# Where stores, halo pages and weight sums stand: a one-core kernel of a hybrid decoder block

## The chip, the cores and the metric

The kernel runs on one core of a Trainium2 chip. The core has a matmul engine (TensorE, PE in the profile), a vector engine (VectorE, DVE), an engine for activation functions (ScalarE, ACT), GpSimd (POOL) and SyncE (SP), from whose queue all transfers of this kernel are issued. The metric is the device time of one launch in microseconds, the lower the better.

## The reference

One layer on a sequence of 2048 positions with 1024 channels, in float32: a mixer of 16 recurrent heads and 8 short-convolution groups, then a gated feed-forward part with a convolution over positions, each with a residual, and a last norm.

```python
def reference(x, norm1_g, w_in, ..., final_g):
    for l in range(DEPTH):
        h = rms_norm(x, norm1_g[l])
        z = jnp.einsum('bsd,de->bse', h, w_in[l])
        lru_x, lru_gate, sc_b, sc_c, sc_x = jnp.split(z, splits, axis=-1)
        lru_x = causal_dwconv(lru_x, lru_conv_w[l]) + lru_conv_b[l]
        y_lru = rg_lru(lru_x, ...) * jax.nn.gelu(lru_gate)
        y_sc = sc_b * causal_dwconv(sc_c * sc_x, sc_conv_w[l])
        y_mix = jnp.concatenate([y_lru, y_sc], axis=-1)
        x = x + jnp.einsum('bse,ed->bsd', y_mix, w_out[l])
        h = rms_norm(x, norm2_g[l])
        u = causal_dwconv(jnp.einsum('bsd,df->bsf', h, w_up[l]), ffn_conv_w[l])
        gate, up = jnp.split(u, 2, axis=-1)
        x = x + jnp.einsum('bsf,fd->bsd', jax.nn.gelu(gate) * up, w_down[l])
    return rms_norm(x, final_g)
```

## The kernel before

Channels lie on the 128 partitions, positions along the free axis. The sequence is worked in two halves of T = 1024 positions, each in two blocks of NB = 512. A float32 value is split into a high and a low part (`split`, L182: ACT rounds, DVE subtracts), and each product is three matmuls. One matmul has a 128x128 weight tile and 512 columns.

The program runs through four kinds of stages, each once for each half: the mixer's input products (`in_phase`, 12 units of the list `UNITS`), the output projection (`project`, two blocks of 12 steps), the up products of the feed-forward part (`up_phase`, 24 pairs of gate `ug` and value `un`), and the down products (`sweeps`). Mixer and projection of half 0 come first, then those of half 1, then up and down of half 0, then up and down of half 1. Up and down use a seven-product scheme for 2x2 blocks: seven sweeps of six steps, each step loading two pages, one of weights or their sums (L756) and one of data (L757), splitting both and issuing 24 matmuls. The sums S1 to S4 of down weights are made early, in `down_sums` (sa, sb, sc), one of twelve beside each unit of half 0's `in_phase`, and spilled to DRAM (`s_d`). The products of the up phase are combined in `up_rest` and spilled to `f_d` (B11 of an even unit alone; of an odd unit B21, B22 and T1 to T4).

What sets the order. TensorE and SP run in the order in which the program is written; DVE, ACT and POOL in an order that a scheduler sets, by priorities. SP's queue is worked in order: a store whose data isn't there holds the loads behind it. Stores therefore don't stand where their data is made: `defer(n, dst, src)` puts them on a list, each load of weights calls `tick`, which counts all down, and a store is issued once it is at the head of the list and its count is 0 or less. So n is the number of weight loads that go ahead of it.

```python
    def tick():
        for w in waiting:
            w[0] -= 1
        while waiting and waiting[0][0] <= 0:
            _, dst, src = waiting.pop(0)
            nc.sync.dma_start(dst, src)
```

Pages. `raw_tile` has two buffers, so a step's load waits until the step two before it is split. Pages of T + 3 columns (`big`) and of two blocks (`res_page`) share four buffers of the tag "u": lru inputs `xl`, the convolution product `pr`, the second half's x, the residuals `xr` of the projection, the h pages `ha` and `hb` of `h_prep`, `ug` and `un` with their halos, and one of the residuals `x2r` of half 0's sweeps ("21"; the others are from the tag "act" with 28 buffers). Sums, h's helpers and up results are from `tmp`, seven buffers.

The stores that matter here: `up_rest` defers its spills by 1, and by 3 for the last two units; `store_pair` defers the second residual stream (x2) and the third (x3, of `down0_done`) by 1; `finish_block` defers the output of half 1 by 1. `h_beside` prepares the h pages of half 1 beside steps 4, 12, 25 and 37 of half 0's sweeps. In half 1's sweeps `down1_beside` loads x3 of half 0 again (fx), scales and stores it, and after step 37 scales the second block of half 1 (L889).

Of the kernel before, what the change touches and what calls it, by code (L numbers as in the profile page):

```python
# [64 lines left out]
def block_kernel(  # L65
# [52 lines left out]
    def tmp(name):  # L118
        return page(name, "tmp", 7)

    def big(name):
        return ub.tile([P, T + 3], F32, name=name, tag="u", bufs=4)

    def raw_tile(name):
        return sb.tile([P, 6, NB], F32, name=name, tag="wr", bufs=2)
# [134 lines left out]
            nc.vector.scalar_tensor_tensor(acc, acc, 1.5, y, ALU.add, ALU.mult)  # L260
        return acc

    def with_halo(name, n, half, store):
        t = big(name)
        if half == 0:
            nc.gpsimd.memset(t[:, 0:n], 0.0)
        else:
            nc.gpsimd.tensor_copy(t[:, 0:n], store)
        return t
# [81 lines left out]
    def sc_first(s, half, acts, rs, ps):  # L351
        cc = flat(act(f"cc{half}_{s}"))
        evac(cc, ps, rs)
        ps = in_product(24 + s, half, acts)
        pr = with_halo(f"pr{half}_{s}", 2, half, p_halo[:, s, :])
        evac(pr[:, 2 : 2 + T], ps, rs)
        nc.vector.tensor_tensor(pr[:, 2 : 2 + T], pr[:, 2 : 2 + T], cc, ALU.mult)
        keep_halo(pr, 2, half, p_halo[:, s, :])
        return pr
# [8 lines left out]
        return cv  # L368

    def x_prep(half, k, parts=1):  # L370
        x = (flat(act(f"x{half}_{k}")) if half == 0 else big(f"x{half}_{k}"))[:, :T]
        hi = flat(act(f"xh{half}_{k}"))
        lo = flat(act(f"xl{half}_{k}"))
        g = col(O_G1 + k)
        n = T // parts
        for i in range(parts):
            ts = slice(i * n, (i + 1) * n)
            nc.sync.dma_start(x[:, ts], xT[k, :, half * T + i * n : half * T + (i + 1) * n])
            nc.scalar.activation(r32(hi[:, ts]), x[:, ts], AF.Copy, scale=g)
            nc.vector.scalar_tensor_tensor(r32(lo[:, ts]), x[:, ts], g, hi[:, ts], ALU.mult, ALU.subtract)  # L380
        return hi, lo, x
# [136 lines left out]
            nc.vector.tensor_tensor(a, a, sq[:, 0, :], ALU.add)  # L518
            nc.vector.tensor_tensor(a, a, sq[:, 1, :], ALU.add)

    def res_page(name):
        return ub.tile([P, 2, NB], F32, name=name, tag="u", bufs=4)

    def x_residual(half):
        def get(t, i):
            r = res_page(f"xr{half}_{t}_{i}")
            o = half * T + t * NB
            nc.sync.dma_start(r, xT[2 * i : 2 * i + 2, :, o : o + NB].rearrange("m p c -> p m c"))
            return r

        return get
# [6 lines left out]

        return get

    def store_pair(dst, t, r):
        defer(1, dst[:, :, blk(t)].rearrange("m p c -> p m c"), r)

    def h_prep(half, k, rs):
        a = big(f"ha{half}_{k}")[:, :T]
        b = big(f"hb{half}_{k}")[:, :T]
        for t, kk in ((a, k), (b, k + 4)):
            nc.sync.dma_start(t, x2_d[half][kk // 2][kk % 2])  # L550
# [46 lines left out]
    class Pair:  # L597
# [66 lines left out]
    def up_rest(half, j, ug, un):  # L664
# [52 lines left out]
    def down_sums(i):  # L717
        a, b, c = tmp(f"sa{i}"), tmp(f"sb{i}"), tmp(f"sc{i}")
        for o, dst in zip(W_OPS, (a[:, 0, :], a[:, 1, :], b[:, 0, :], b[:, 1, :])):
            nc.sync.dma_start(dst, w_down[W_OPS.index(o), i // 2].rearrange("p (k c) -> p k c", k=2)[:, i % 2, :])  # L720
# [289 lines left out]
```

## Time and profile before

| | |
|---|---|
| three runs | 2390.15, 2395.49, 2396.87 us, median 2395.49 |
| profiled execution | 2394.19 us, of which the span of the trace is 2392.4 |
| granted TensorE clock, mean | 0.987 |
| matmuls | 10128 |
| data moved | 349.99 MB, mean 146 GB/s |

The stages on TensorE, from its lines in the trace: in_phase 0 to 347 and 486 to 814, project 347 to 486 and 814 to 946, up_phase(0) 946 to 1404, sweeps(0) 1404 to 1662, up_phase(1) 1662 to 2120, sweeps(1) 2120 to 2375, the last norm and stores to 2392.

A row of a timeline has the start, the length, engine, line, operation, what it writes and reads, and in brackets how long its engine stood idle before it and what ended that. "SPq" is SP's issue of a transfer: its length includes the wait for the data. A row on stretches has the busy time and number of instructions of PE, PE's weight loads, DVE, ACT and POOL, then the clock that TensorE was granted, the share of the DMA engines, and GB/s. A row on waits has the total, the number and the longest.

### The profile page before, as it was taken

To read this page: it belongs to the slowest core of one execution; us is meant where nothing else is said; L and a number is where in the kernel's file an instruction comes from. 1 tells how busy PE (TensorE), PEld (TensorE's weight loads), DVE (VectorE), ACT (ScalarE), POOL (GpSimd) and SP (SyncE) were. 2 spreads that over 40 slices of the span, in tenths; PEclk is the share of its full clock that TensorE was granted. 3 is DMA by queue.
4 is the path that set the end of the run, shared out by engine and by line. 5 is a ranking of instruction groups with operands and counts; after the bars stand their busy time and mean duration, and the time that the engine had idled before them with its cause. 6 is when DMAs were issued, how large, how long until landed. Compare 5 with 4: busy or idle time off the path is not lost.

```text
span 2392.4 us, 26345 instructions
## 1 busy us (share of the span) xinstructions
PE 2323.6 (97%) x10128; PEld 1912.8 (80%) x10128; DVE 1695.5 (71%) x1890; ACT 1128.4 (47%) x1254; POOL 146.9 (6%) x194
## 2 busy tenths in 40 slices
PE   8999999999999999999999999999999999999995
PEld 7788878888888888888888878777888888877883
DVE  6766665566655767888888877557887888766555
ACT  5563454445553634544444444344544544433442
POOL 0000000000000000111111100001111111100000
PEclk9999999999999999999999999999999999999997
DMA  4343446632222555223333256555223323268653
GB/s 165 126 145 134 163 178 215 241 102 66 71 69 64 182 216 209 84 88 118 107 106 110 88 198 246 205 182 211 84 93 120 106 100 110 88 215 311 216 195 123
DMA packets 141183, 349.99 MB, mean 146 GB/s; under 512 B 13056, under 2 KB 16256, under 8 KB 141056
## 3 DMA queue, kind: packets, MB, share of 16 engines
q1 hardware_dynamic: 141056, 348.30, 41.4%
q8 instruction: 79, 1.29, 0.2%
q14 instruction: 48, 0.39, 0.1%
HBM read 258.07 MB, written 90.18 MB: 146 GB/s over the span
## 4 chain that ended last, share of the span: by engine, by line
PE 78%; DVE 6%; DMA 4%; ACT 3%; issue 1%; SPq 1%; POOL 0%; DVEq 0%; ACTq 0%; POOLq 0%
PE zx L608 22%; PE zin_b L222 13%; PE zc L608 11%; PE o L189 10%; PE dx L745 8%; PE dy L745 8%; PE za L608 5%; DMA wr_in<-in_w_in 1%; DMA wr_d<-f_d_B 1%; DVE x2r L782 1%; DVE cv L282 1%; DVE fl_d L184 1%; DVE r L334 1%; DMA s_dS<-sc 1%; SPq L180 1%
## 5 line engine op out<-in xcount | busy, mean ns | idle before, releaser
L222 PE MATMUL zin_b<-xh,wh_in 128*128 128x512 f32 x896 | 277.2, 390 | 4.6 <-DVE ss_a L258 2.6
L222 PE MATMUL zin_b<-xl,wh_in 128*128 128x512 f32 x896 | 277.3, 390 | 0.1
L222 PE MATMUL zin_b<-xh,wl_in 128*128 128x512 f32 x896 | 276.3, 390 | 0.0
L189 PE MATMUL o<-yb_o,wh_o 128*128 128x512 f32 x768 | 238.8, 392 | 2.5 <-DVE yb_o L184 1.6
L222 PEld LDWEIGHTS zin_b<-xh,wh_in 128*128 128x128 f32 x896 | 168.8, 188 | 40.8 <-DVE ss_a L258 3.5
L222 PEld LDWEIGHTS zin_b<-xl,wh_in 128*128 128x128 f32 x896 | 168.4, 188 | 36.5 <-DVE xl L380 1.8
L222 PEld LDWEIGHTS zin_b<-xh,wl_in 128*128 128x128 f32 x896 | 168.7, 188 | 35.0
L184 DVE TENSOR_TENSOR fl_d<-wr_d,fh_d 128x1024 fp32r<-128x1024 f32 x84 | 102.8, 1224 | 109.4 <-ACT fh_d L183 106.9
L745 PE MATMUL dx<-fh_d,wh_d 128*128 128x512 f32 x384 | 153.3, 399 | 27.4 <-ACT fh_d L183 27.4
L189 PEld LDWEIGHTS o<-yb_o,wh_o 128*128 128x128 f32 x768 | 145.3, 189 | 33.9 <-DVE yb_o L184 2.0
L183 ACT ACTIVATE fh_d<-wr_d 128x1024 fp32r<-128x1024 f32 x84 | 89.2, 1062 | 163.1 <-PE dy L745 80.8
L184 DVE TENSOR_TENSOR wla_up<-wr_up,wha_up 128x1024 fp32r<-128x1024 f32 x48 | 58.8, 1226 | 143.7 <-ACT wha_up L183 143.7
L745 PE MATMUL dx<-fl_d,wh_d 128*128 128x512 f32 x384 | 154.6, 403 | 6.1 <-DVE fl_d L184 6.1
L189 PE MATMUL o<-yb_o,wl_o 128*128 128x512 f32 x384 | 150.9, 393 | 3.0 <-DVE wl_o L184 3.0
L745 PE MATMUL dx<-fh_d,wl_d 128*128 128x512 f32 x384 | 152.9, 398 | 0.0
L184 DVE TENSOR_TENSOR wl_d<-wr_d,wh_d 128x1024 fp32r<-128x1024 f32 x84 | 102.6, 1222 | 64.6 <-ACT wh_d L183 62.1
L183 ACT ACTIVATE wh_in<-wr_in 128x1024 fp32r<-128x1024 f32 (+1 forms) x62 | 60.3, 975 | 175.7 <-DMA wr_in<-in_w_in 175.7
L183 ACT ACTIVATE wh_d<-wr_d 128x1024 fp32r<-128x1024 f32 x84 | 88.6, 1055 | 112.7 <-DMA wr_d<-in_w_down 56.7
L584 DVE TENSOR_TENSOR wr_up<-wr_up 128x512 f32<-128x512 f32 x192 | 130.3, 687 | 9.2 <-DMA wr_up<-in_w_up 8.0
L184 DVE TENSOR_TENSOR wl_in<-wr_in,wh_in 128x1024 fp32r<-128x1024 f32 (+1 forms) x62 | 69.2, 1119 | 86.1 <-ACT wh_in L183 82.9
L608 PE MATMUL zc<-hhB,whd_up 128*128 128x512 f32 x384 | 126.0, 389 | 0.0
L282 DVE SCALAR_TENSOR_TENSOR cu<-un,prm,cu 128x1024 f32<-128x1024 f32 x96 | 122.8, 1279 | 4.3 <-ACT cu L278 4.3
(238 smaller groups left out, 5351.7 us busy)
## 6 DMA issues: line engine op xcount, KB each, us to landing
wr_up<-in_w_up SPq DMA_DIRECT2D x96, 512.0 KB, 4.8
wr_in<-in_w_in SPq DMA_DIRECT2D x54, 512.0 KB, 4.2
wr_o<-in_w_out SPq DMA_DIRECT2D x24, 1024.0 KB, 7.0
wr_d<-s_dS SPq DMA_DIRECT2D x48, 512.0 KB, 3.7
wr_d<-f_d_T SPq DMA_DIRECT2D x48, 512.0 KB, 4.8
f_d_B<-cu SPq DMA_DIRECT2D x72, 256.0 KB, 2.2
wr_d<-in_w_down SPq DMA_DIRECT2D x36, 512.0 KB, 4.0
wr_d<-f_d_B SPq DMA_DIRECT2D x36, 512.0 KB, 4.6
```

The costliest lines, as they stand in the source:

```text
L180: nc.sync.dma_start(dst, src)
L183: nc.scalar.activation(r32(hi), src, AF.Copy)
L184: nc.vector.tensor_tensor(r32(lo), src, hi, ALU.subtract)
L189: nc.tensor.matmul(ps, r32(a), r32(b), start=(first and i == 0), stop=(last and i == 2))
L222: nc.tensor.matmul(ps[t], r32(a), r32(b[:, blk(t)]), start=(first and i == 0), stop=(last and i == 2))
L282: nc.vector.scalar_tensor_tensor(dst, src[:, k : k + T], col(o_w + k), dst, ALU.mult, ALU.add)
L334: nc.vector.tensor_tensor_scan(h, a, i, init, ALU.mult, ALU.add)
L584: nc.vector.tensor_tensor(raw[:, o, :], raw[:, a, :], raw[:, b, :], ALU.add)
L608: nc.tensor.matmul(ps, r32(p[:, s]), r32(self.hs[k][x][o]), start=f and i == 0, stop=l and i == 2, skip_group_check=True,)
L745: nc.tensor.matmul(ps[m], r32(p), r32(x[:, k, :]), start=first and i == 0 and n == 0, stop=(last or not on_x) and i == ni - 1 and n == 2, ...
L782: nc.vector.tensor_tensor(r, r, ps[m], ALU.add if sign > 0 else ALU.subtract)
```

## The change

Six edits, all of order and place; what is computed, and the number of instructions on TensorE, stay.

1. `up_rest`: the spills of unit 22 are still deferred by 3, those of unit 23 by 6.
2. `store_pair` takes a count; the x3 stores are deferred by 4, those of the last result "21" by 2.
3. `finish_block` defers the output stores by 4, and the kernel's end empties the list.
4. The tag "u" of four buffers becomes "a" and "b" of two each. ug, pr, both h pages and the residual "21" take a; un and the residual "12" (from "act" before) take b; xl, the second half's x and xr alternate.
5. `sums_at`: sums 0 to 5 run beside units 3 to 8 of half 0, sums 6 to 11 beside units 3 to 8 of half 1.
6. The last h pages of half 1 are prepared beside step 34 instead of 37.

```diff
@@ big and res_page
-        return ub.tile([P, T + 3], F32, name=name, tag="u", bufs=4)
+        return ub.tile([P, T + 3], F32, name=name, tag="ab"[side], bufs=2)
...
-        xl = with_halo(f"xl{half}_{c}", 3, half, xl_halo[:, c, :])
+        xl = with_halo(f"xl{half}_{c}", 3, half, xl_halo[:, c, :], c % 2)
...
-            r = res_page(f"xr{half}_{t}_{i}")
+            r = res_page(f"xr{half}_{t}_{i}", i % 2)
...
+    def store_pair(dst, t, r, when=1):
+        defer(when, dst[:, :, blk(t)].rearrange("m p c -> p m c"), r)
...
-        a = big(f"ha{half}_{k}")[:, :T]
-        b = big(f"hb{half}_{k}")[:, :T]
+        a = big(f"ha{half}_{k}", 0)[:, :T]
+        b = big(f"hb{half}_{k}", 0)[:, :T]
...
-            self.ug = with_halo(f"ug{n}", 2, self.half, u_halo[:, self.j, :])
-            self.un = with_halo(f"un{n}", 2, self.half, u_halo[:, NFF + self.j, :])
+            self.ug = with_halo(f"ug{n}", 2, self.half, u_halo[:, self.j, :], 0)
+            self.un = with_halo(f"un{n}", 2, self.half, u_halo[:, NFF + self.j, :], 1)
...
-        when = 1 if j < NFF - 2 else 3
+        when = {NFF - 2: 3, NFF - 1: 6}.get(j, 1)
...
+    def sums_at(first, i0, also=None):
+        def between(n):
+            if also is not None:
+                also(n)
+            if first <= n < first + NI // 2:
+                down_sums(i0 + n - first)
+
+        return between
...
-    in_phase(0, None, ss1[0], down_sums)
+    in_phase(0, None, ss1[0], sums_at(3, 0))
...
-    in_phase(1, x1, ss1[1], late_mean(ss2[0], "b0", rs2[0], 1))
+    in_phase(1, x1, ss1[1], sums_at(3, NI // 2, late_mean(ss2[0], "b0", rs2[0], 1)))
...
-        store_pair(x3_d[2 * mh + m // 2], t, r)
+        store_pair(x3_d[2 * mh + m // 2], t, r, 2 if key == "21" else 4)
...
-        down_residual(0, lambda key, n: res_page(n) if key == "21" else act(n)),
+        down_residual(0, lambda key, n: res_page(n, "21 12".split().index(key)) if key in ("21", "12") else act(n)),
         down0_done,
-        h_beside(1, (4, 12, 25, 37)),
+        h_beside(1, (4, 12, 25, 34)),
...
-                defer(1, yT[c : c + 2, :, o : o + NB].rearrange("m p c -> p m c"), r)
+                defer(4, yT[c : c + 2, :, o : o + NB].rearrange("m p c -> p m c"), r)
...
-    tick()
+    while waiting:
+        tick()
```

SP's queue at the start of half 0's sweeps. wr_d_0_3 is the load of sweep 0, step 3; L756 and L757 of before are L765 and L766 of the change; cu_22 to tt_23 are the results of the last two up units. Before:

```order
L756 DMA wr_d_0_2_10091<-in_w_down 128x1024
L757 DMA wr_d_0_2_10091<-f_d_B_2_111 128x1024
L180 DMA f_d_B_5_114<-cu_22_9900 128x512
L180 DMA f_d_B_5_120<-cu_23_9992 128x512
L180 DMA f_d_B_5_126<-cu_23_9992 128x512
L180 DMA f_d_T_5_132<-cg_23_9991 128x512
L180 DMA f_d_T_5_138<-cg_23_9991 128x512
L180 DMA f_d_T_5_144<-tt_23_10001 128x512
L180 DMA f_d_T_5_150<-tt_23_10001 128x512
L756 DMA wr_d_0_3_10133<-in_w_down 128x1024
L757 DMA wr_d_0_3_10133<-f_d_B_3_112 128x1024
L756 DMA wr_d_0_4_10168<-in_w_down 128x1024
```

and in the change:

```order
L765 DMA wr_d_0_2_10091<-in_w_down 128x1024
L766 DMA wr_d_0_2_10091<-f_d_B_2_111 128x1024
L180 DMA f_d_B_5_114<-cu_22_9900 128x512
L765 DMA wr_d_0_3_10127<-in_w_down 128x1024
L766 DMA wr_d_0_3_10127<-f_d_B_3_112 128x1024
L765 DMA wr_d_0_4_10162<-in_w_down 128x1024
L766 DMA wr_d_0_4_10162<-f_d_B_4_113 128x1024
L550 DMA ha_0_10197<-x_d_0_221 128x1024
L550 DMA hb_0_10198<-x_d_2_223 128x1024
L765 DMA wr_d_0_5_10224<-in_w_down 128x1024
L766 DMA wr_d_0_5_10224<-f_d_B_5_114 128x1024
L180 DMA f_d_B_5_120<-cu_23_9992 128x512
```

The six stores of unit 23 (two from cu_23, two from cg_23, two from tt_23; the first of them is the last row here) moved from ahead of the load of step 3 to behind that of step 5. Half 1's sweeps begin in the same way, with the fx pages in the place of ha and hb.

SP's queue in sweep 5 of half 0, where the residual "22" is stored; wr_d_5_1 is the load of sweep 5, step 1. Before:

```order
L756 DMA wr_d_5_0_11219<-s_dS_0_211 128x1024
L757 DMA wr_d_5_0_11219<-f_d_B_0_121 128x1024
L180 DMA x_d_227<-x2r_22_0_10323 128x2x512
L180 DMA x_d_228<-x2r_22_1_10325 128x2x512
L756 DMA wr_d_5_1_11256<-s_dS_1_212 128x1024
L757 DMA wr_d_5_1_11256<-f_d_B_1_122 128x1024
L756 DMA wr_d_5_2_11291<-s_dS_2_213 128x1024
```

and in the change:

```order
L765 DMA wr_d_5_0_11219<-s_dS_0_211 128x1024
L766 DMA wr_d_5_0_11219<-f_d_B_0_121 128x1024
L765 DMA wr_d_5_1_11254<-s_dS_1_212 128x1024
L766 DMA wr_d_5_1_11254<-f_d_B_1_122 128x1024
L765 DMA wr_d_5_2_11289<-s_dS_2_213 128x1024
L766 DMA wr_d_5_2_11289<-f_d_B_2_123 128x1024
L765 DMA wr_d_5_3_11324<-s_dS_3_214 128x1024
L766 DMA wr_d_5_3_11324<-f_d_B_3_124 128x1024
L180 DMA x_d_227<-x2r_22_0_10323 128x2x512
L180 DMA x_d_228<-x2r_22_1_10325 128x2x512
L765 DMA wr_d_5_4_11361<-s_dS_4_215 128x1024
```

The two stores moved from behind the first load of the sweep to behind the fourth. The stores of "11" in sweep 4 and of "12" in sweep 6 moved alike.

DVE's order in the last sweep of half 1. wl_d_6_3 and fl_d_6_3 are the low parts of weights and data of sweep 6, step 3; rl_l and L258 to L260 are the norm of the second block, L889 (L898 in the change) the scaling of the output. Before:

```order
L184 TENSOR_TENSOR rl_l_16438<-ss_l_14969,rh_l_16437 128x512
L258 SCALAR_TENSOR_TENSOR ss_l_14969<-ms_l_0_16441,ry_l_16444 128x512
L259 SCALAR_TENSOR_TENSOR ss_l_14969<-ss_l_14969,ry_l_16444 128x512
L260 SCALAR_TENSOR_TENSOR ss_l_14969<-ss_l_14969,ry_l_16444 128x512
L889 SCALAR_TENSOR_TENSOR x2r_12_0_15263<-x2r_12_0_15263,prm,ss_l_14969 128x512 x2
L889 SCALAR_TENSOR_TENSOR x2r_12_1_15265<-x2r_12_1_15265,prm,ss_l_14969 128x512 x2
L889 SCALAR_TENSOR_TENSOR x2r_22_0_15267<-x2r_22_0_15267,prm,ss_l_14969 128x512 x2
L889 SCALAR_TENSOR_TENSOR x2r_22_1_15269<-x2r_22_1_15269,prm,ss_l_14969 128x512 x2
L184 TENSOR_TENSOR wl_d_6_3_16500<-wr_d_6_3_16496,wh_d_6_3_16499 128x1024
L184 TENSOR_TENSOR fl_d_6_3_16504<-wr_d_6_3_16496,fh_d_6_3_16503 128x1024
L184 TENSOR_TENSOR wl_d_6_4_16535<-wr_d_6_4_16531,wh_d_6_4_16534 128x1024
L184 TENSOR_TENSOR fl_d_6_4_16539<-wr_d_6_4_16531,fh_d_6_4_16538 128x1024
```

and in the change:

```order
L184 TENSOR_TENSOR rl_l_16438<-ss_l_14969,rh_l_16437 128x512
L184 TENSOR_TENSOR wl_d_6_3_16496<-wr_d_6_3_16492,wh_d_6_3_16495 128x1024
L184 TENSOR_TENSOR fl_d_6_3_16500<-wr_d_6_3_16492,fh_d_6_3_16499 128x1024
L258 SCALAR_TENSOR_TENSOR ss_l_14969<-ms_l_0_16441,ry_l_16444 128x512
L259 SCALAR_TENSOR_TENSOR ss_l_14969<-ss_l_14969,ry_l_16444 128x512
L184 TENSOR_TENSOR wl_d_6_4_16531<-wr_d_6_4_16527,wh_d_6_4_16530 128x1024
L260 SCALAR_TENSOR_TENSOR ss_l_14969<-ss_l_14969,ry_l_16444 128x512
L898 SCALAR_TENSOR_TENSOR x2r_12_0_15263<-x2r_12_0_15263,prm,ss_l_14969 128x512 x2
L184 TENSOR_TENSOR fl_d_6_4_16535<-wr_d_6_4_16527,fh_d_6_4_16534 128x1024
L184 TENSOR_TENSOR wl_d_6_5_16546<-wr_d_6_5_16538,wh_d_6_5_16545 128x1024
L898 SCALAR_TENSOR_TENSOR x2r_12_1_15265<-x2r_12_1_15265,prm,ss_l_14969 128x512 x2
L898 SCALAR_TENSOR_TENSOR x2r_22_0_15267<-x2r_22_0_15267,prm,ss_l_14969 128x512 x2
```

The splits of step 3 moved ahead of the norm, and those of steps 4 and 5 in between the scalings (fl_d_6_5 stands behind six of the eight).

More of the change, by code (lines that the diff above doesn't have):

```diff
@@ L119, in tmp, with big @@
         return page(name, "tmp", 7)
-    def big(name):
-        return ub.tile([P, T + 3], F32, name=name, tag="u", bufs=4)
+    def big(name, side):
+        return ub.tile([P, T + 3], F32, name=name, tag="ab"[side], bufs=2)
     def raw_tile(name):
@@ L261, in inv_rms, with with_halo @@
         return acc
-    def with_halo(name, n, half, store):
-        t = big(name)
+    def with_halo(name, n, half, store, side):
+        t = big(name, side)
         if half == 0:
@@ L354, in sc_first @@
         ps = in_product(24 + s, half, acts)
-        pr = with_halo(f"pr{half}_{s}", 2, half, p_halo[:, s, :])
+        pr = with_halo(f"pr{half}_{s}", 2, half, p_halo[:, s, :], 0)
         evac(pr[:, 2 : 2 + T], ps, rs)
@@ L370, in x_prep @@
     def x_prep(half, k, parts=1):
-        x = (flat(act(f"x{half}_{k}")) if half == 0 else big(f"x{half}_{k}"))[:, :T]
+        x = (flat(act(f"x{half}_{k}")) if half == 0 else big(f"x{half}_{k}", k % 2))[:, :T]
         hi = flat(act(f"xh{half}_{k}"))
@@ L519, in add_squares, with res_page @@
             nc.vector.tensor_tensor(a, a, sq[:, 1, :], ALU.add)
-    def res_page(name):
-        return ub.tile([P, 2, NB], F32, name=name, tag="u", bufs=4)
+    def res_page(name, side):
+        return ub.tile([P, 2, NB], F32, name=name, tag="ab"[side], bufs=2)
     def x_residual(half):
         def get(t, i):
-            r = res_page(f"xr{half}_{t}_{i}")
+            r = res_page(f"xr{half}_{t}_{i}", i % 2)
             o = half * T + t * NB
@@ L539, in x2_residual @@
         return get
-    def store_pair(dst, t, r):
-        defer(1, dst[:, :, blk(t)].rearrange("m p c -> p m c"), r)
+    def store_pair(dst, t, r, when=1):
+        defer(when, dst[:, :, blk(t)].rearrange("m p c -> p m c"), r)
     def h_prep(half, k, rs):
-        a = big(f"ha{half}_{k}")[:, :T]
-        b = big(f"hb{half}_{k}")[:, :T]
+        a = big(f"ha{half}_{k}", 0)[:, :T]
+        b = big(f"hb{half}_{k}", 0)[:, :T]
         for t, kk in ((a, k), (b, k + 4)):
```

## The prediction

> **What bounds the kernel now.** I read the page's busy shares first, then the waits of the matmul engine, then stretches of 20 us, and last the queue of SP around each hole. The page and the list of TensorE's waits:
>
> ```profile
> PE 2323.6 (97%) x10128; PEld 1912.8 (80%) x10128; DVE 1695.5 (71%) x1890; ACT 1128.4 (47%) x1254; POOL 146.9 (6%) x194
> PE dx L745 <- ACT fh_d L183: 27.4, 5, 12.5
> PE dy L745 <- ACT fh_d L183: 4.2, 1, 4.2
> ```
>
> TensorE is the bound, and the count of its matmuls does not change. So the only time to be had is where it stands still or runs at the lower clock. Six waits in the down sweeps hold 31.6 us of it, all for the split of a freshly loaded page. Counting matmuls in stretches shows the whole price, the slow restart included (columns: stretch, its length, busy us and instructions of PE, PEld, DVE, ACT, POOL, granted clock, DMA share, GB/s):
>
> ```profile
> 1400.00:1420.00 20.00, 20.00 (x90) 16.57 (x89) 13.26 (x14) 5.87 (x6) 1.11 (x1) 1.00 0.30 101
> 340.00:360.00 20.00, 16.50 (x60) 12.92 (x59) 19.19 (x22) 7.07 (x9) 2.62 (x2) 0.83 0.86 321
> 420.00:440.00 20.00, 18.95 (x83) 15.06 (x82) 14.56 (x18) 10.71 (x14) 0.00 (x0) 1.00 0.99 363
> 1420.00:1440.00 20.00, 15.30 (x61) 11.97 (x60) 16.42 (x16) 11.37 (x12) 0.00 (x0) 0.91 0.83 305
> 1540.00:1560.00 20.00, 15.72 (x61) 12.31 (x60) 14.96 (x19) 9.25 (x10) 0.00 (x0) 0.91 0.75 271
> 1580.00:1600.00 20.00, 15.37 (x56) 11.87 (x55) 9.40 (x10) 8.48 (x9) 0.00 (x0) 0.83 0.74 263
> 1620.00:1660.00 40.00, 34.31 (x136) 27.17 (x135) 30.11 (x33) 19.08 (x19) 7.45 (x2) 0.91 0.64 237
> 2120.00:2140.00 20.00, 17.17 (x76) 13.89 (x74) 11.82 (x13) 5.09 (x5) 0.00 (x0) 1.00 0.44 153
> 2140.00:2160.00 20.00, 18.12 (x72) 14.65 (x73) 12.52 (x12) 8.49 (x8) 0.00 (x0) 0.91 0.98 359
> 2160.00:2180.00 20.00, 18.31 (x81) 14.84 (x80) 11.62 (x11) 6.07 (x6) 0.00 (x0) 1.00 0.92 340
> 2200.00:2220.00 20.00, 19.47 (x86) 15.83 (x85) 13.22 (x11) 8.08 (x8) 0.00 (x0) 1.00 0.85 312
> 2340.00:2367.00 27.00, 13.40 (x48) 9.95 (x47) 14.56 (x17) 6.36 (x6) 0.00 (x0) 0.75 0.54 195
> ```
>
> A quiet stretch holds 89 or 90 matmuls, so I take 20/89.5 = 0.2235 us for one, and 24 of them, one step of a sweep, as 5.36 us. What is missing gives each hole: **at 340** 29.5 matmuls, 6.6 us; **A** (1420) 28.5, 6.4; **B** (1540) 28.5, 6.4; **C** (1580) 33.5, 7.5; **D** (1620 to 1660) 43, 9.6; **E** (2120 and 2140) 13.5 + 17.5, 6.9; **F** (2160 and 2200) 8.5 + 3.5, 2.7; **G** (2340 to 2367, where 121 would fit) 73, 16.3. Together 62.4 us. In most of these stretches the clock is granted at 0.75 to 0.91, so part of each is paid after the wait is over: A waits 3.94 us (row below) and loses 6.4.
>
> **Why the holes are there.** SP's queue around A and B, the vector work that its stores wait for, and the first matmul after each hole:
>
> ```profile
> 1396.65 17.45 SPq L180 DMA_DIRECT2D f_d_B<-cu  x3
> 1416.59 0.48 SPq L756 DMA_DIRECT2D wr_d<-in_w_down  x1
> 1415.23 0.69 DVE L687 SCALAR_TENSOR_TENSOR tt<-cg,cu 128x512 f32<-128x512 f32 x1
> 1424.45 0.50 PE L745 MATMUL dx<-fh_d,wh_d 128*128 128x512 f32 x1 [3.94 <-ACT fh_d L183]
> 1527.30 0.32 SPq L756 DMA_DIRECT2D wr_d<-s_dS  x1
> 1539.46 2.73 DVE L782 TENSOR_TENSOR x2r<-x2r,dy 128x512 f32<-128x512 f32 x4 [1.31 <-PE dy L745]
> 1540.85 1.73 SPq L180 DMA_DIRECT2D x_d<-x2r  x2
> 1542.69 0.44 SPq L756 DMA_DIRECT2D wr_d<-s_dS  x1
> 1550.42 0.50 PE L745 MATMUL dx<-fh_d,wh_d 128*128 128x512 f32 x1 [3.52 <-ACT fh_d L183]
> ```
>
> A store whose data isn't there holds everything behind it. At A the three f_d_B stores sit 17.45 us until the last up unit's product is made, and the next weight load goes out at 1416.59; TensorE gets its data 1424.45 − 1416.59 = 7.9 us later. At B it is 1550.42 − 1542.69 = 7.7. So **a load must be issued 7.8 us before TensorE needs it**. How early does it go unhindered? At B TensorE wanted the page at 1550.42 − 3.52 = 1546.90, so it began the step before at 1546.90 − 5.36 = 1541.54, and that step's load had gone out at 1527.30: 14.2 us ahead, a slack of 14.2 − 7.8 = **6.4 us**.
>
> **The change part by part.**
>
> *Last spills (A, E).* Behind the load of step 2 now stands the B11 store of unit 22 alone, ready when the old queue reached the group (1396.65). Unit 23's six stores stand behind the load of step 5. Step 3 begins at about 1424.45 − 3.94 = 1420.5, step 5 at 1431.2, its load goes out at 1431.2 − 14.2 = 1417.0, and the last product is ready at 1415.23 + 0.69 = 1415.9: nothing waits, with 1.1 us in hand and 6.4 of slack behind. A loses 6.4, E (the same rows one half later) 6.9. What is late next is traffic: six stores of 128x512 f32, 6 x 262144 bytes = 1.57 MB, now leave beside h or fx pages. At the 359 GB/s of the stretch at 2140 that is 4.4 us for the load behind, inside the slack. I keep 0.5 us at A, 1.0 at E, 1.5 at F; bounds 0 and all of it.
>
> *x3 stores (B, C, D).* They stand four loads on. At B the load now freed goes out at 1546.90 − 14.2 = 1532.7, the third after it 10.7 us later at 1543.4, and only then comes the store, whose data is complete at 1539.46 + 2.73 = 1542.2. So it finds its data with 1.2 us to spare and 6.4 of slack behind. I keep 0.5 us in each of the three; bounds 0 and the whole hole.
>
> *Final stores (G).* SP, DVE and TensorE of before:
>
> ```profile
> 2341.93 5.39 DVE L889 SCALAR_TENSOR_TENSOR x2r<-x2r,prm,ss_l 128x512 f32<-128x512 f32 x8
> 2343.37 4.35 SPq L180 DMA_DIRECT2D out_yT<-x2r  x4
> 2347.81 0.46 SPq L756 DMA_DIRECT2D wr_d<-in_w_down  x1
> 2355.62 0.79 PE L745 MATMUL dx<-fh_d,wh_d 128*128 128x512 f32 x1 [12.54 <-ACT fh_d L183]
> ```
>
> Four yT stores stood ahead of the last three loads and waited for the eight scalings. Now the loads stand ahead, and on DVE the splits of step 39 come before the norm's chain, those of 40 and 41 between the scalings. A split then waits for at most two scalings of 5.39/8 = 0.67 us, and TensorE's last two steps are held until a split of step 41 that stands behind six of them. I keep 1.5 us (bounds 0 and 6, half of what eight scalings and a slow clock cost). The end behind the last matmul is untouched.
>
> *Weight sums (340).* The twelve sums ran one per unit in half 0, the last beside the projection's first loads. SP's first load of the projection in half 0, then in half 1, where no sums were, and three stretches:
>
> ```profile
> 336.71 0.43 SPq L449 DMA_DIRECT2D wr_o<-in_w_out  x1
> 793.90 0.43 SPq L449 DMA_DIRECT2D wr_o<-in_w_out  x1
> 44.00:64.00 20.00, 13.94 (x57) 10.33 (x56) 17.35 (x22) 9.18 (x9) 1.40 (x3) 0.99 0.33 105
> 70.00:340.00 270.00, 270.00 (x1193) 223.62 (x1192) 174.43 (x185) 140.48 (x144) 11.94 (x22) 1.00 0.41 141
> 814.00:834.00 20.00, 20.00 (x90) 16.57 (x89) 19.96 (x23) 10.01 (x12) 0.00 (x0) 1.00 0.87 315
> ```
>
> Half 0 starts projecting at 347, half 1 at 814, so the lead is 10 us against 20, and half 1 starts with a full 90 matmuls. With the last sums at unit 8, I keep 0.3 of 6.6. In return six units of half 1 carry sums. In half 0 units with sums ran from 70 to 340 without a hole (1193 matmuls are 0.226 us each) and left DVE a third of its time. I charge 0.5 us, bounds 0 and 19 (below). The hole at 44 (57 matmuls) loses two sums in DVE's order and gains two loads in SP's, by the order of the units: 0, and as bounds a fifth of its 7.3 us either way, −1.5 and +1.5.
>
> *Page pairs.* With ug and un bound to their own pairs, a ug page comes free with the last read of cg's convolution rather than of cu's, and the first ug of half 1 takes the page of a residual whose store must land.
>
> ```profile
> 1751.36 1.65 POOL L268 COPY un<-u_halo 128x2 f32<-128x2 f32 x1 [3.08 <-DVE cg L282]
> 1756.49 0.60 ACT L619 ACTIVATE ug<-zx 128x512 f32<-128x512 f32 x1 [2.20 <-PE zx L608]
> 1662.54 1.58 SPq L180 DMA_DIRECT2D x_d<-x2r  x2
> 1665.54 0.19 POOL L268 COPY ug<-u_halo 128x2 f32<-128x2 f32 x1 [18.00 <-DMA x_d<-x2r]
> 1544.04 0.48 SPq L550 DMA_DIRECT2D ha<-x_d  x1
> 1561.01 1.22 DVE L184 TENSOR_TENSOR hlB<-hb,hhB 128x1024 fp32r<-128x1024 f32 x1
> ```
>
> A ug page freed as un's is now would be there at 1751.36 + 0.49 and is wanted at 1756.49: 4.6 us in hand, cost 0. The first ug of half 1 would be there at 1665.7, and TensorE needs it copied only two products (24 matmuls, 5.4 us) after its start at 1662: about 1 us in hand, cost 0, bounds 0 and 3. An h page is held 1562.2 − 1544.0 = 18.2 us; the residual "21" now takes the pages of h34 three steps (16.1 us) later, so SP waits 2 us, inside the slack. For pages handed on later in the second projection I charge 1.0 us, bounds 0 and 3.
>
> **The sum.** Kept of the 62.4: 0.3 at 340, 0.5 at A, 1.5 in B to D, 1.0 at E, 1.5 at F and 1.5 at G, together 6.3. New: 0.5 for the sums and 1.0 for the pages. Gain 62.4 − 6.3 − 1.5 = 54.6. The profiled execution took 2394.19 with a span of 2392.4; 2394.2 − 54.6 = 2339.6, rounded **2340** (that execution lies 1.3 below the median of the runs shown, which I leave out).
>
> **The rivals.**
>
> *Only part returns, because the DMA engines are full.* For: 2140 to 2180 moves 359 and 340 GB/s at shares of 0.98 and 0.92, and the stretch at 420 shows 363 at 0.99 with 83 matmuls. The stretch at 2120 moves only 153, and what is unblocked can fill it: (359 − 153) x 20 us = 4.1 MB, more than the spills. Against it: the spills now come after the loads. If bandwidth holds the sweeps' starts, A, E and F keep 14 of 16 us, 11 more than I keep: 2351; with half of B to D back as well (11.8 − 1.5), 2361. Chance 0.16. The Trainium skill's page "DMA: Bandwidth & Descriptors", section "Where 436 GB/s comes from", gives about 358 GB/s as the HBM limit of a core, and 363 here agrees. By it the 17.0 MB that 2120 to 2180 move need 47.6 us, so that stretch could shrink by 12.4 at most, and the forecast takes 7.1.
>
> *The stores block again, further on.* The queue ahead now runs earlier, and the margins are 1.1 and 1.2 us. If a step's data comes 1.2 + 6.4 = 7.6 us later than I place it, B, C and D return whole: 23.5 − 1.5 = 22 us, 2362. Below that it costs nothing. This is also how the change would not do what it says. Chance 0.05.
>
> *New waits in half 1's mixers.* Sums share seven pages with two accumulators there. SP's waits in half 0 have 11 for stores of earlier sums, longest 3.1:
>
> ```profile
> SPq L720 <- DMA s_dS<-sc: 14.2, 11, 3.1
> ```
>
> If each of six reached TensorE whole, 19 us: 2359. Against it: the same units in half 0 carried the same without a hole (the row of 70 to 340). Chance 0.08.
>
> *Slower.* The gate's halo pages become the bound in the up phase: 48 units, each waiting for its ug page. It decides when that page comes 4.6 + 54.6/48 = 5.7 us later than placed; at 2 us beyond the slack in each unit it is 96 us, 2436. Against it: POOL is busy 6%, and two pages a stream are what the four gave alternately. Chance 0.02.
>
> **How the numbers follow.** Forecast 0.69, rivals 0.16, 0.05, 0.08 and 0.02. All kept residues gone and the early holes better gives 2340 − 6.3 − 1.5 − 1.5 = 2331; the upper end takes in the new waits and the full rivals of bandwidth, 2362. Some 0.3%, 7 us, is about what a measurement tells from no change. The first four cases are all far faster, with what is unforeseen: faster 0.96, within 0.02, slower 0.02.
>
> **What would show it.** Stretches at A to E with 86 or more matmuls and a clock of 1.00; no L180 row longer than 2 us ahead of a weight load in the sweeps, except for fx; TensorE's waits for fh_d under 3 us in all instead of 31.6; the projection's first load some 20 us ahead in half 0. Holes again at the sweeps' starts with a DMA share of 0.95 speak for the first rival; L180 rows of 10 us for the second; POOL's ug copy right before an ACT wait for the last. I am wrong if waits for fh_d stay above 10 us or new ones appear before 946.

## The result and the profile after

The changed kernel takes **2334.40 us** (median of 4 runs, 2333.31 to 2335.79) against 2394.77 for the kernel before on the same chip: a ratio of 0.9751, 95% interval 0.9734 to 0.9768. The prediction was 2340, with a range from 2331 to 2362. On a second chip the same kernel was run again as a control: 2333.86, ratio 0.9737 (0.9724 to 0.9750).

The span of the profiled execution fell by 59.7 us, from 2392.4 to 2332.7, at the same 10128 matmuls. TensorE's line of the page and its longest waits after:

```profile
PE 2306.0 (99%) x10128; PEld 1903.2 (82%) x10128; DVE 1693.3 (73%) x1890; ACT 1125.5 (48%) x1254; POOL 135.7 (6%) x194
PE zin_b L222 <- DVE ss_a L258: 2.6, 1, 2.6
PE zin_b L222 <- ACT xh L379: 2.6, 2, 1.5
PE dy L754 <- DVE fl_d L184: 1.9, 1, 1.9
```

No wait for fh_d is left in the list, where there were 31.6 us. Stretches of the changed kernel that answer to the holes of before:

```profile
340.00:360.00 20.00, 20.00 (x90) 16.57 (x89) 16.30 (x17) 8.82 (x10) 1.22 (x2) 1.00 0.78 269
1420.00:1440.00 20.00, 20.00 (x90) 16.57 (x89) 14.03 (x15) 9.22 (x10) 0.00 (x0) 1.00 0.81 297
1540.00:1560.00 20.00, 20.00 (x90) 16.57 (x89) 14.95 (x16) 11.37 (x13) 0.00 (x0) 1.00 0.60 209
1580.00:1600.00 20.00, 20.00 (x90) 16.53 (x89) 19.64 (x24) 13.45 (x14) 0.00 (x0) 1.00 0.76 264
1620.00:1660.00 40.00, 40.00 (x178) 33.14 (x177) 30.93 (x39) 17.52 (x22) 3.01 (x4) 1.00 0.26 91
2100.00:2120.00 20.00, 18.08 (x75) 14.51 (x74) 9.71 (x11) 5.50 (x6) 0.00 (x0) 0.94 1.04 372
2280.00:2307.00 27.00, 26.25 (x117) 21.41 (x116) 22.70 (x29) 13.78 (x16) 0.00 (x0) 1.00 0.58 215
```

Full stretches of 90 matmuls at a clock of 1.00 (178 in the one of 40 us) stand where 56 to 61 stood (136 in the one of 40). Of the large holes one is left, at the start of half 1's sweeps (2100 to 2120: 75 matmuls, a clock of 0.94), with the DMA engines full. SP's queue after, first at the start of half 0's sweeps, then in sweep 4, then the first load of the projection; and TensorE's first matmul of that projection:

```profile
1408.19 0.33 SPq L765 DMA_DIRECT2D wr_d<-in_w_down  x1
1408.57 0.43 SPq L766 DMA_DIRECT2D wr_d<-f_d_B  x1
1409.05 0.91 SPq L180 DMA_DIRECT2D f_d_B<-cu  x2
...
1528.41 0.32 SPq L765 DMA_DIRECT2D wr_d<-s_dS  x1
1528.78 0.43 SPq L766 DMA_DIRECT2D wr_d<-f_d_T  x1
1529.25 0.95 SPq L180 DMA_DIRECT2D x_d<-x2r  x2
...
323.35 0.39 SPq L449 DMA_DIRECT2D wr_o<-in_w_out  x1
343.96 0.62 PE L189 MATMUL o<-yb_o,wh_o 128*128 128x512 f32 x2
```

The stores that took 17.45 and 1.73 us after a long silence now take 0.91 and 0.95 right behind their load: their data is there. The projection's load has a lead of 20.6 us.

To compare many runs I sum by place how much further apart the matmuls start than 0.2267 us, the distance from one to the next where nothing disturbs them. That is all the time TensorE loses, slow clock included: 82.8 us before, 23.4 after, so 59.4 of the 59.7 us are found. By place, for this and the runs below (us):

| run | early, 44 to 76 | hole at 347 | half 1's projection | start of half 0's sweeps (A) | sweep 4 (B) | sweep 5 (C) | sweep 6 (D) | half 1's first sweeps (E, F) | last sweep (G) | all |
|---|---|---|---|---|---|---|---|---|---|---|
| before | 8.8 | 6.7 | 1.5 | 6.7 | 6.4 | 7.6 | 9.4 | 9.5 | 16.5 | 82.8 |
| after | 5.7 | 0 | 2.1 | 0 | 0 | 0 | 0 | 4.6 | 1.0 | 23.4 |
| e1_spills3 | 5.7 | 0 | 3.3 | 7.7 | 0 | 0 | 0 | 10.1 | 1.0 | 37.9 |
| e2_x3at1 | 5.7 | 0 | 1.8 | 0 | 6.1 | 7.5 | 6.2 | 5.2 | 1.0 | 43.5 |
| e3_out1 | 5.7 | 0 | 1.6 | 0 | 0 | 0 | 0.7 | 5.1 | 15.7 | 38.6 |
| e4_sums0 | 7.5 | 8.8 | 4.3 | 0 | 0 | 0 | 0 | 4.6 | 1.0 | 35.6 |
| e5_onepool | 5.7 | 0 | 4.4 | 0 | 0 | 0 | 0.5 | 5.1 | 1.0 | 26.6 |
| e6_near | 5.9 | 0 | 1.4 | 5.6 | 5.4 | 0.1 | 8.1 | 5.5 | 1.0 | 42.4 |
| e8_nearclear | 5.7 | 0 | 1.7 | 0.7 | 0 | 1.4 | 7.6 | 4.3 | 1.0 | 31.8 |
| e9_sums6 | 5.7 | 2.1 | 1.4 | 0 | 0 | 0 | 0 | 3.4 | 1.0 | 23.5 |
| e7_fxlater | 5.7 | 0 | 1.3 | 0 | 0 | 0 | 0 | 1.5 | 1.0 | 17.9 |
| e10_fxlater2 | 5.7 | 0 | 2.3 | 0 | 0 | 0 | 0 | 0 | 1.0 | 19.3 |

What is not in a column is the start, 4.5 to 5.7 us, the end, 3.0, some 1.5 in half 0's projection, and single rows of 0.3 or less.

### The profile page after: what moved, and what is told of

Read it like the earlier page. It is cut to its first block, busy times and chain, and to the rows that moved or that the text cites. A ratio compares the mean times of both kernels' runs of the same rounds, so it can differ in the third digit from the quotient of the medians.

```text
span 2332.7 us, 26351 instructions
## 1 busy us (share of the span) xinstructions
PE 2306.0 (99%) x10128; PEld 1903.2 (82%) x10128; DVE 1693.3 (73%) x1890; ACT 1125.5 (48%) x1254; POOL 135.7 (6%) x194
## 4 chain that ended last, share of the span: by engine, by line
PE 95%; DVE 3%; DMA 1%; ACT 1%; issue 0%; SPq 0%; DVEq 0%; ACTq 0%
PE zin_b L222 26%; PE zx L608 22%; PE zc L608 11%; PE o L189 11%; PE dx L754 9%; PE dy L754 8%; PE za L608 6%; PE zi_b L222 1%; PE zr_b L222 1%; DMA wr_d<-s_dS 0%; DVE x2r L791 0%; DVE x2r L898 0%; DMA wr_o<-y_d 0%; DMA fx<-x_d 0%; DVE fl_d L184 0%
## 5 line engine op out<-in xcount | busy, mean ns | idle before, releaser
L754 PE MATMUL dx<-fl_d,wh_d 128*128 128x512 f32 x384 | 149.6, 390 | 1.3 <-DVE fl_d L184 1.3
L282 DVE SCALAR_TENSOR_TENSOR cg<-ug,prm,cg 128x1024 f32<-128x1024 f32 x96 | 122.9, 1280 | 0.7
```

Source lines behind the costliest of these rows:

```text
L282: nc.vector.scalar_tensor_tensor(dst, src[:, k : k + T], col(o_w + k), dst, ALU.mult, ALU.add)
L754: nc.tensor.matmul(ps[m], r32(p), r32(x[:, k, :]), start=first and i == 0 and n == 0, stop=(last or not on_x) and i == ni - 1 and n == 2, ...
```

## The experiments

All but the control c_after are the changed kernel with the lines shown edited further. The kernel before took 2397.8 us beside e1 to e4, 2397.0 beside e5 to e7 and 2396.6 beside the rest.

**Each edit taken back.** Spills, x3 stores, output stores and sums:

```diff
e1_spills3
-        when = {NFF - 2: 3, NFF - 1: 6}.get(j, 1)
+        when = 1 if j < NFF - 2 else 3
e2_x3at1
-        store_pair(x3_d[2 * mh + m // 2], t, r, 2 if key == "21" else 4)
+        store_pair(x3_d[2 * mh + m // 2], t, r)
e3_out1
-                defer(4, yT[c : c + 2, :, o : o + NB].rearrange("m p c -> p m c"), r)
+                defer(1, yT[c : c + 2, :, o : o + NB].rearrange("m p c -> p m c"), r)
e4_sums0
-    in_phase(0, None, ss1[0], sums_at(3, 0))
+    in_phase(0, None, ss1[0], down_sums)
...
-    in_phase(1, x1, ss1[1], sums_at(3, NI // 2, late_mean(ss2[0], "b0", rs2[0], 1)))
+    in_phase(1, x1, ss1[1], late_mean(ss2[0], "b0", rs2[0], 1))
```

> The changed kernel with the spills of unit 23 deferred by 3 again, all else as changed. My theory (a store that waits holds the loads behind it): the holes at the starts of both sweeps are back, 6.5 us at 1420 and 6.8 at 2100, less the 3.8 us that the burst costs there now: 2334.4 + 9.5 = about 2344, with an f_d_B row of 17 to 18 us in SP's queue. Rival (the other edits took the pressure off, so the place of these stores no longer matters): within 2 us of 2334.

Measured 2347.71 us (ratio 0.9791, 0.9776 to 0.9805). Both holes are back, 7.7 and 5.5 us more; the other 1.3 of the 14.5 us more that this execution loses lie mostly in half 1's projection. SP's row has the length of the one of before:

```profile
1388.90 17.45 SPq L180 DMA_DIRECT2D f_d_B<-cu  x3
```

> The changed kernel with the x3 stores deferred by 1 again. Theory: the holes B, C and D come back at their old price, 6.4 + 7.5 + 9.6 = 23.5, so 2358, with TensorE waits for fh_d of about 3.5 to 4.2 us three times. D may be smaller (6.5), since h's last pages are no longer prepared beside it: then 2355. Rival (stores at one load's distance are hidden once the pages come from pairs): under 2340.

Measured 2354.97 (0.9820, 0.9806 to 0.9835): the three holes, 19.8 us together. D is 6.2 and not 9.4, as it may be without h pages beside it.

> The changed kernel with the output stores of finish_block deferred by 1 again. Theory: the hole of the last sweep comes back, 16.3 less the 1.0 that is left of it now: 2334.4 + 15.3 = about 2350, with the eight scalings in one piece on DVE and a wait of 12 us for fh_d. Rival (the scheduler's order on DVE, not SP's queue, made that hole, and it stays good): under 2340.

Measured 2349.26 (0.9797, 0.9782 to 0.9812). DVE's eight scalings are one piece again and TensorE waits 12.3 us. The scalings, that wait, the first load behind the four stores, and DVE's first split after the scalings:

```profile
2297.75 5.39 DVE L898 SCALAR_TENSOR_TENSOR x2r<-x2r,prm,ss_l 128x512 f32<-128x512 f32 x8
PE dx L754 <- ACT fh_d L183: 12.3, 1, 12.3
2303.63 0.46 SPq L765 DMA_DIRECT2D wr_d<-in_w_down  x1
2309.56 1.23 DVE L184 TENSOR_TENSOR wl_d<-wr_d,wh_d 128x1024 fp32r<-128x1024 f32 x1 [6.43 <-ACT wh_d L183]
```

So the scheduler's order on DVE moves with the place of four stores on SP's queue. What ends the wait is the load: DVE is through with the scalings at 2303.14 and then stands idle for 6.43 us, until the weights loaded from 2303.63 on are there and ACT has rounded them. What the order on DVE alone would cost, with the loads in time, no run shows.

> The changed kernel with all twelve sums beside the units of half 0 again. Theory: the hole at 347 is back (6.7) and the early hole at 58 to 67 too (3.1 more than now), and what half 1 pays for sums (0.5) goes: 2334.4 + 9.3 = about 2344. Rival (the pairs of pages, not the sums, took away the one or the other): 2338 to 2341, with only one of the two holes back.

Measured 2341.60 (0.9762, 0.9745 to 0.9778); its runs spread from 2339.1 to 2347.1, and the profiled one is the slowest. In that one the hole at 347 is 8.8 us, where 6.7 were expected, the early one is 1.8 more than in the changed kernel and not 3.1, and half 1's projection loses 4.3, which was not expected and is not explained. The median lies 3.5 to 6.9 us above 0.9751 and 0.9737 of this chip's 2397.8, the profiled execution loses 12.2 more than the changed kernel's, so the size of this edit is known no better than between these. The mechanism is tried further in e9.

**Pages.** The four-buffer tag, and h's last pages at 37:

```diff
e5_onepool
-        return ub.tile([P, T + 3], F32, name=name, tag="ab"[side], bufs=2)
+        return ub.tile([P, T + 3], F32, name=name, tag="u", bufs=4)
...
-        return ub.tile([P, 2, NB], F32, name=name, tag="ab"[side], bufs=2)
+        return ub.tile([P, 2, NB], F32, name=name, tag="u", bufs=4)
...
-        down_residual(0, lambda key, n: res_page(n, "21 12".split().index(key)) if key in ("21", "12") else act(n)),
+        down_residual(0, lambda key, n: res_page(n, 0) if key == "21" else act(n)),
...
-        h_beside(1, (4, 12, 25, 34)),
+        h_beside(1, (4, 12, 25, 37)),
```

> The changed kernel without the pairs: one tag of four buffers for all halo, h and residual pages, residual 12 from the other pool again, h's last pages beside step 37 again; deferrals and sums stay as changed. My theory: the pairs are worth little, 0 to +2 us (2334 to 2337), since the same pages free in the same order but for the last h pages. Rival A (the pairs are what lets the x3 stores stand far back, or their pages collide with the residuals): a hole of 5 us or more at 1600 to 1665, 2340 or more. Rival B (pairs cost something in half 1's projection): 1 us faster.

Measured 2335.86 (0.9746, 0.9732 to 0.9759), not to be told from the changed kernel's 0.9751 and 0.9737. Taken back together, the pairs and the earlier h pages are worth nothing that shows; half 1's projection lost 4.4 us in this execution, but between 1.3 and 4.3 with pairs in others.

**How far back must a store stand?**

```diff
e6_near
-        when = {NFF - 2: 3, NFF - 1: 6}.get(j, 1)
+        when = {NFF - 2: 3, NFF - 1: 4}.get(j, 1)
...
-        store_pair(x3_d[2 * mh + m // 2], t, r, 2 if key == "21" else 4)
+        store_pair(x3_d[2 * mh + m // 2], t, r, 1 if key == "21" else 2)
e8_nearclear, beside these two lines
-        h_beside(1, (4, 12, 25, 34)),
+        h_beside(1, (9, 14, 28, 34)),
```

> The changed kernel with shorter distances: spills of unit 23 deferred by 4 instead of 6, x3 stores by 2 instead of 4 (the last by 1 instead of 2). My theory is a threshold: a load is issued 14.2 us before it is wanted and needs 7.8, and a store that stands one load further on lets that load go, so the load behind it comes 1.5 to 1.8 us ahead of need. Then nothing or little is lost: 2334 to 2338. Rival (each load of distance is worth its share, the wait only shrinks by 5.4 us per load or the slack isn't there): a third to a half of the 33 us of these holes is back, 2345 or more.

Measured 2354.02 (0.9819, 0.9806 to 0.9833): my expectation failed by 16 us, and the time is one that the rival named (2345 or more). But the holes are not alike: 5.6, 5.4 and 8.1 us at A, B and D, and 0.1 at C. SP's queue and TensorE at B, then SP's at C and TensorE's stretch there:

```profile
1529.92 1.73 SPq L180 DMA_DIRECT2D x_d<-x2r  x2
1531.69 0.51 SPq L550 DMA_DIRECT2D ha<-x_d  x1
1532.24 0.82 SPq L550 DMA_DIRECT2D hb<-x_d  x1
1533.17 0.43 SPq L765 DMA_DIRECT2D wr_d<-s_dS  x1
1543.43 0.49 PE L754 MATMUL dx<-fh_d,wh_d 128*128 128x512 f32 x1 [2.03 <-ACT fh_d L183]
...
1568.00 1.73 SPq L180 DMA_DIRECT2D x_d<-x2r  x2
1569.83 0.44 SPq L765 DMA_DIRECT2D wr_d<-s_dS  x1
1565.00:1585.00 20.00, 20.00 (x90) 16.53 (x90) 12.09 (x14) 7.42 (x8) 0.00 (x0) 1.00 0.68 244
```

At B two h pages (1 MB) go between the store and the load, and the load needs 1543.43 − 1533.17 = 10.3 us to TensorE instead of 7.8. At C the load comes right behind the store, and all but 0.1 us is hidden. So the time from load to matmul, which I had taken from rows with nothing ahead of the load, was wrong for a queue with pages in it.

> The short distances of the run before (spills of unit 23 by 4, x3 by 2, the last by 1), and h's pages beside steps 9, 14, 28 and 34 instead of 4, 12, 25 and 34, so that no h page stands between a waiting store and the next load at 1405 and 1530. My theory now: the short distance failed there because 1 MB of pages went ahead of the load (it then needed 10 us to TensorE, not 7.8), and where nothing stood between (sweep 5) 0.1 us was lost. So the holes at 1416 to 1436 (5.6) and 1541 to 1548 (5.4) fall to 1 us or less each and the one at 1612 (8.1, residual pages between) stays: 10 us faster than the short distances alone, 2343. Rival (the distance itself is too short whatever stands between): both holes stay, 2352 to 2354.

Measured 2345.32 (0.9787, 0.9773 to 0.9800), 8.7 us faster than e6_near on another chip (the kernels before differ by 0.4 there), with 0.7 us left at A and none at B. At C 1.4 us appear, though the load goes out right behind the store, at 1561.56: TensorE begins on it at 1569.34, 7.8 us later, and waits 0.76 us more for the low part of the data. At D the residual pages still stand between:

```profile
1595.78 1.55 SPq L871 DMA_DIRECT2D x2r<-x_d  x2
1597.44 0.50 SPq L765 DMA_DIRECT2D wr_d<-in_w_down  x1
1607.37 0.79 PE L754 MATMUL dx<-fh_d,wh_d 128*128 128x512 f32 x1 [4.06 <-ACT fh_d L183]
```

Again 1607.37 − 1597.44 = 9.9 us. A store two loads back is only just far enough if a load follows it at once (0.1 and 1.4 us lost at C, none at B); four loads cover 1 MB of other pages as well.

**Where the sums stand.**

```diff
e9_sums6
-    in_phase(0, None, ss1[0], sums_at(3, 0))
+    in_phase(0, None, ss1[0], sums_at(6, 0))
...
-    in_phase(1, x1, ss1[1], sums_at(3, NI // 2, late_mean(ss2[0], "b0", rs2[0], 1)))
+    in_phase(1, x1, ss1[1], sums_at(6, NI // 2, late_mean(ss2[0], "b0", rs2[0], 1)))
```

> The changed kernel with the sums beside units 6 to 11 of both halves instead of 3 to 8. Theory (the hole at 347 comes from the last sums' pages and stores ahead of the projection's first loads): it is back in half 0 (6.7 to 8.8 us) and a new one of that size appears in half 1 at about 808, early waits between 58 and 67 stay small: 2334 + 14 = 2348. Rival (twelve sums in one half were simply too many for DMA and DVE, six anywhere are hidden): 2334 to 2337.

Measured 2335.96 (0.9748, 0.9735 to 0.9762), against 2333.86 of the control. The time is the rival's (2334 to 2337). Of the theory's two holes of 7 us, 2.1 us stand at 345 to 350 and nothing in half 1, so neither mechanism held whole. SP's rows and TensorE's start in half 0, then in half 1:

```profile
331.58 0.43 SPq L449 DMA_DIRECT2D wr_o<-in_w_out  x1
343.94 0.61 PE L189 MATMUL o<-yb_o,wh_o 128*128 128x512 f32 x2
791.22 0.38 SPq L449 DMA_DIRECT2D wr_o<-in_w_out  x1
806.33 0.62 PE L189 MATMUL o<-yb_o,wh_o 128*128 128x512 f32 x2
```

The lead is 12.4 us there and 15.1 here; it was 347.0 − 336.7 = 10.3 before, at a loss of 6.7, and is 20.6 in the changed kernel. So the sums beside the last units shorten the lead, and the loss begins at a lead somewhere between 12.4 and 15.1 us; but that the sums of units 0 to 5 shorten it by 2 us more, as they did before, is seen and not explained. Nor is the lead all of it: in e9_sums6 ACT has rounded the first weights at 340.92, but DVE makes their low part (wl_o) only at 344.08, behind a scan and a product, and it is for wl_o that TensorE waits first, 0.80 us at 345.35. No run parts the load's lead from DVE's order here.

**What is left at 2114.** In the changed kernel, SP, ACT, DVE and TensorE there:

```profile
2101.62 1.16 SPq L765 DMA_DIRECT2D wr_d<-s_dS  x1
2110.24 1.06 ACT L183 ACTIVATE wh_d<-wr_d 128x1024 fp32r<-128x1024 f32 x1 [6.25 <-DMA wr_d<-s_dS]
2112.48 2.47 DVE L791 TENSOR_TENSOR x2r<-x2r,dx 128x512 f32<-128x512 f32 x4
2114.87 1.22 DVE L184 TENSOR_TENSOR fl_d<-wr_d,fh_d 128x1024 fp32r<-128x1024 f32 x1
2116.14 0.50 PE L754 MATMUL dy<-fl_d,wh_d 128*128 128x512 f32 x1 [1.92 <-DVE fl_d L184]
```

ACT can begin on the load 8.6 us after its issue, and then four residual additions stand ahead of the split that TensorE waits for. Two edits move the x3 reloads (fx) of half 1 out of this crowd:

```diff
e7_fxlater
-        if s >= 4 and s % 4 == 0 and s // 4 <= KC // 2:
-            i = s // 4 - 1
+        if s >= 9 and s % 4 == 1 and s // 4 <= KC // 2 + 1:
+            i = s // 4 - 2
e10_fxlater2
-        if s >= 4 and s % 4 == 0 and s // 4 <= KC // 2:
-            i = s // 4 - 1
+        if s >= 14 and s % 4 == 2 and s // 4 <= KC // 2 + 2:
+            i = s // 4 - 3
```

> The changed kernel with the four reloads of x3 (fx) beside steps 9, 13, 17 and 21 of half 1's sweeps instead of 4, 8, 12 and 16. My theory: what is left at 2114 to 2121 (3.8 us) is traffic: spills, fx, and four residual pages in the same 20 us (372 GB/s at a share of 1.04). Without fx there it shrinks to 1 us or less: 2331.5. Rival (the loss is DVE's, four residual additions ahead of the split that TensorE waits for, whatever the traffic): stays at 3 us or more there, 2334.

Measured 2330.37 (0.9724, 0.9711 to 0.9738); the hole is gone; 1.5 us are lost at 2161, where the changed kernel lost 0.8 at 2157.

> The changed kernel itself, as the measure for the others on this chip. 2333 to 2338, by the spread between chips seen for the kernel before (2394.8 to 2397.8).

Measured 2333.86, as told above.

> The changed kernel with the reloads of x3 beside steps 14, 18, 22 and 26 of half 1's sweeps. If only the crowd in the first eight steps costs (theory), any place behind it does as well as steps 9 to 21 did: no hole over 1.5 us between 2100 and 2170, 5 us faster than the changed kernel on the same chip. If the stores of fx themselves hold loads wherever they stand (rival), holes of 1 us or more appear at 2150 to 2230, up to four of them, and the gain is 2 us or less.

Measured 2329.31 (0.9721, 0.9707 to 0.9734), 4.6 us faster than the control on its chip, with no hole left there. The stretch at 2100 in e7_fxlater, then in e10_fxlater2, and there the load and ACT's start on it:

```profile
2100.00:2120.00 20.00, 20.00 (x90) 16.57 (x89) 11.32 (x12) 8.38 (x8) 0.00 (x0) 1.00 1.02 371
```

```profile
2100.00:2120.00 20.00, 20.00 (x90) 16.57 (x89) 10.84 (x12) 6.66 (x7) 0.00 (x0) 1.00 1.01 366
2100.24 0.59 SPq L765 DMA_DIRECT2D wr_d<-s_dS  x1
2106.61 1.06 ACT L183 ACTIVATE wh_d<-wr_d 128x1024 fp32r<-128x1024 f32 x1 [2.27 <-DMA wr_d<-s_dS]
```

The DMA engines are as full in these 20 us as in the changed kernel, yet TensorE runs through: what counts is that the bytes ahead of the weight loads are fewer (no fx pages and no stores of them), not the rate. ACT can begin 6.4 us after the issue and not 8.6. The four additions are there in both runs, so alone they don't make the hole. All five runs of e10_fxlater2 are faster than all four of the changed kernel on its chip. e7_fxlater ran on a chip without that control; its ratio of 0.9724 stands against 0.9751 and 0.9737.

## Why the prediction was right, step by step

*The mechanism.* A store that waits for its data at the head of SP's queue starves TensorE a few steps on. Held: each of the three edits that move stores, taken back alone, brought its holes back at about their old price (e1, e2, e3); in e3 the order on DVE moved with them, and the load was what ended the wait.

*Spills and x3 stores.* Held, and the margins of 1.1 and 1.2 us were enough: nothing of A to D is left, where I kept 2.0. The slack under it was too large. I had a load reach TensorE 7.8 us after its issue; that is right only when no other page goes ahead of it, and 10 us otherwise (e6, e8). With that time only 4 us or so of the slack of 6.4 are there. It did no harm at a distance of four loads.

*Traffic behind the spills.* I kept 1.0 at E and 1.5 at F, thinking 4.4 us of stores inside the slack; 3.8 and 0.8 are left, and the sign that I had named, 86 matmuls or more at a clock of 1.00, fails at E alone (75 at 0.94). These two terms were too small by 2.1 us. The rival of full DMA engines shows in this one place, for 3.8 of the 14 us that it keeps, and e7 and e10 lose nothing there with the engines as full: the bytes ahead of the loads made it. The Trainium skill's page "DMA: Bandwidth & Descriptors", section "Where 436 GB/s comes from", gives about 358 GB/s as the HBM limit of a core; 20 us at 372 were seen here.

*Final stores.* Kept 1.5, measured 1.0.

*Sums.* The lead of 20 us came as forecast (20.6), and the hole is gone. Half 1 pays nothing that shows. The step that was mis-sized is the early hole: I put it at 0 within 1.5 us either way, and it fell by 3.1. Before, sums stood on DVE between the steps of the first gate's chain, at 55.98, 57.78 and, right ahead of the split that TensorE waits for, at 60.97; in the changed kernel there are none. The last of the sums and TensorE's start before, then its start in the changed kernel:

```profile
60.97 0.68 DVE L722 TENSOR_TENSOR sc<-sa,sb 128x512 f32<-128x512 f32 x1
62.84 0.73 PE L222 MATMUL zr_b<-xcl,gw 128*128 128x512 f32 x2 [1.31 <-DVE xcl L184]
61.40 0.73 PE L222 MATMUL zr_b<-xcl,gw 128*128 128x512 f32 x2 [0.50 <-DVE xcl L184]
```

The loss at 60 to 67 fell by 4.7 us, from 5.5 to 0.8. At 47, where TensorE waits 2.64 us in both, 1.6 came on top, because there the clock fell in the changed kernel and not before (last section). Whether the change does that or chance, one trace of the kernel before can't tell; e8_nearclear loses 3.3 there too.

*Pages.* No cost in the up phase, as forecast: ug's page is freed by cg's convolution, and neither ACT nor TensorE waits for it.

```profile
1711.89 1.63 POOL L268 COPY ug<-u_halo 128x2 f32<-128x2 f32 x1 [3.11 <-DVE cg L282]
1717.00 0.60 ACT L619 ACTIVATE ug<-zx 128x512 f32<-128x512 f32 x1 [2.20 <-PE zx L608]
```

The copy is done at 1713.52, 3.5 us ahead of need. I had 4.6, with 0.49 us for a copy whose row has 1.65. I charged 1.0 in half 1's projection and 0.6 is there, which is within the spread of that place. By e5 these edits bring nothing that shows either.

*The sum.* 54.6 forecast, 59.7 measured. The 5.1 us between are the early hole (3.1), A to D (2.0), charges of 1.5 of which 0.6 came, 0.3 at 340 and 0.5 at G, less 2.1 at E and F. The last 0.4 is that the holes of before come to 62.8 us by the starts of the matmuls, where I counted 62.4. So the sum is close partly because misses of both signs stand in it.

## What to carry to other kernels

Where one queue issues loads and stores in order, a store belongs behind as many loads as its data is late, and the distance that is needed must be counted in bytes ahead of the next load, not in loads alone. Count matmuls in equal stretches before and after: it prices a hole with its slow restart, which the list of waits puts too low. Before a queue is made shorter, look for what will then meet in the same 20 us.

## What the runs showed of the hardware

TensorE's clock can fall after waits of 2 us, and doesn't always. In e6_near the waits at 1541 to 1546 are 2.03 (its row stands above) and 1.48 us and cost 5.4; the longest at 1429 to 1436 is 1.80, and 3.7 are lost. The second of the one and the last of the other, and the two stretches:

```profile
1545.41 0.80 PE L754 MATMUL dx<-fl_d,wh_d 128*128 128x512 f32 x1 [1.48 <-DVE fl_d L184]
1430.89 0.50 PE L754 MATMUL dy<-fl_d,wh_d 128*128 128x512 f32 x1 [1.80 <-DVE fl_d L184]
1540.00:1560.00 20.00, 16.49 (x66) 13.01 (x65) 15.42 (x17) 11.97 (x13) 0.00 (x0) 0.91 0.55 201
1420.00:1440.00 20.00, 17.35 (x69) 13.49 (x68) 17.13 (x19) 10.91 (x12) 0.00 (x0) 0.91 0.77 283
```

The granted clock is 0.91 in both, and from 1432.5 to 1435.5 the matmuls stand 0.43 us apart instead of 0.2267. The Trainium skill's page "TensorE: Matmul & The Clock Gate", part 1, has the clock halved after an idle window of about 3.4 us; here it dropped after less. But the length of the wait alone doesn't decide. In e9_sums6 a longer one cost little more than itself, 2.6 us, at a clock of 1.00:

```profile
2117.84 0.50 PE L754 MATMUL dy<-fl_d,wh_d 128*128 128x512 f32 x1 [2.31 <-DVE fl_d L184]
2100.00:2120.00 20.00, 17.68 (x78) 14.32 (x77) 10.91 (x12) 6.36 (x6) 0.00 (x0) 1.00 1.03 360
```

And the same wait of 2.64 us at 47 cost 3.3 us in the kernel before, at a clock of 1.00 from 40 to 60, and 4.9 in the changed kernel, at 0.91. So in these runs a wait of about 2 us was paid between once and twice; what decides between them stays open.
